# One scan chain in the S5 stage, more buffers there, adaLN by TensorE alone, and the convolutions of q, k and v where their projections end

## The chip, the core and the metric

The kernel runs on one core of one Trainium2 chip. The metric is the time of one execution on the device in microseconds (us). The core's engines are TensorE (PE, matmul), its weight load (PEld), VectorE (DVE), ScalarE (ACT), GpSimd (POOL) and SyncE (SP, which issues most DMAs). Each engine carries out its own instructions in one fixed order and waits on semaphores for the others.

## The reference, cut to what matters

One layer of a diffusion trunk: 512 latent tokens and 256 context tokens of width 2048, all float32.

```
mod = silu(c) @ ada_w + ada_b                    # adaLN, 6 parts of 2048
hin = concat([ctx*(1+csc1)+csh1, x*(1+sc1)+sh1]) # 768 tokens
proj = hin @ w_in                                # u | q | k | v | z | a,b
s5   = s5_mixer(u)      # 64 groups, bidirectional diagonal complex scan, gelu, gate
q, k, v = silu(short_conv(q,k,v))                # 5 taps along the tokens, per channel
dn   = gated_delta_rule(l2norm(q), l2norm(k), v) # 8 heads of 128, chunks of 64, both directions
x = layer_norm(ALPHA*x + g1 * (concat(s5, rms(dn)*silu(z)) @ w_out))
x = layer_norm(ALPHA*x + g2 * expert_choice_ffn(x*(1+sc2)+sh2))   # 16 experts, SwiGLU
```

The context tokens enter through the scans only; the output is the latent stream. g1, sh2, sc2 and g2 are four of the six adaLN parts, 2048 columns each, made in 16 chunks of 512 columns.

## The kernel before, in words

Matrix products that must be exact to float32 are made by splitting a weight tile in two: `split_w` (L380) loads `wr` by DMA, casts it to `wh` on ACT (L388) and subtracts to get `wl` on POOL (L390); `mm3` (L394) then makes three matmuls, L396 to L398. `proj_store` (L422) uses this for one head of q, k, v or z: 16 steps of 128 rows, 512 latent columns in the PSUM tile `pl` and, for k and v, 256 context columns in `pc`, copied by ACT to a tile `ue` and sent to DRAM (`pj`).

The program runs through these stages. `phase_in` makes the first adaLN parts and the S5 inputs u, which `put_u` sends to DRAM. The S5 stage follows: `s5_lags` (L1104 and others, mostly DVE), `s5_states` (matmuls L1133, 32 steps of two groups), `s5_scan` (94 dependent steps of three DVE operations, L1156 to L1158; `CHAINS` cuts the 64 groups into chains that are scanned apart), `s5_local`, `s5_outputs` (16 steps: two ACT copies `Hs`, L1188 and L1189, then 16 matmuls, L1192), `s5_gelu`, and `gates` (ends in six transposes, L495). The projections of k and v for 8 heads and the first six of q and z (`PRE`) stand after it in the source; the tool that sets each engine's order mixes their matmuls into the S5 stage, wherever it expects PE to be free.

Then the DeltaNet stage: ten iterations, in each of which `merge` interleaves `dn_front` for one head, `dn_inverse` and `dn_values` for the head before, `dn_scan` for the one before that, and up to four of the remaining projections (`REST`: four of q, six of z). `dn_front` and `dn_values` load the raw k, q, v from `pj` and call `conv_silu`: one ACT scaling, four DVE multiply-adds (L511) for each part, one ACT tanh and one DVE multiply (L514). The first PE work of the stage is L572, the transposes of the finished k of head 0. The same stretch holds the S5 gate product, the output projection (`mix_parts`) and the adaLN chunks that are left. `ada_rest` makes 16 chunks; four are made early (`NN`), of which two by `ada_vec`, on DVE, and 12 come in the DeltaNet stage. Each chunk by `ada_chunk` is 8 DMAs of 512 KB and 16 matmuls (L217) of 512 columns with 32 weights each, in four groups of PE columns.

The rest of the program, from L1370 on (router, experts, final norm), is bound by PE and by the experts' weights, and the change does not touch it.

Of the kernel before, what the change touches and what calls it, by code (L numbers as in the profile page):

```python
# [11 lines left out]
F32 = mybir.dt.float32  # L12
# [193 lines left out]
def ada_chunk(K, I, pool, c0, nk=8, bufs=2):  # L206

    nc = K.nc
    src = I["ada_w"]
    pa = mp(K, (128, 512), K.adb)  # L210
    for k0 in range(0, KT, nk):
        aw = pool.tile([128, nk, 512], F32, name="aw", tag="aw", bufs=bufs)
        nc.sync.dma_start(aw, ap(src, c0 + k0 * 128 * 6 * D, [[6 * D, 128], [128 * 6 * D, nk], [1, 512]]))
        for kk in range(nk):
            k = k0 + kk
            j = k % 4
            nc.tensor.matmul(pa[32 * j:32 * j + 32], K.cT[:, k], aw[:, kk], start=k < 4, stop=k >= 12, tile_position=(0, 32 * j))  # L217
    return pa
# [12 lines left out]
def ada_cols(K, I, pool, c0, dst, m, **kw):  # L231

    nc = K.nc
    pa = ada_chunk(K, I, pool, c0, **kw)
    pm = mp(K, (128, 512), K.adb)[:, :4 * m].rearrange("p (a b) -> p a b", a=4)
    turn(K, pool, pa, pm)
    cb = c0 // 128
    nc.vector.tensor_tensor(dst, pm, bc(K.cols[:, cb:cb + 4][:, :, None], [128, 4, m]), op=ADD)
    yield from ()


def ada_vec(K, I, pool, c0, dst, m, nk, bufs):

    nc = K.nc
    V = nc.vector
    acc = pool.tile([128, 512], F32, name="part2", bufs=1)
    for k0 in range(0, KT, nk):
        aw = pool.tile([128, nk, 512], F32, name="aw", tag="aw", bufs=bufs)
        nc.sync.dma_start(aw, ap(I["ada_w"], c0 + k0 * 128 * 6 * D, [[6 * D, 128], [128 * 6 * D, nk], [1, 512]]))
        for kk in range(nk):  # L250
            c = K.cT[:, k0 + kk, 0:1]
            if k0 + kk == 0:
                V.tensor_scalar(acc, aw[:, kk], c, None, op0=MUL)
            else:
                V.scalar_tensor_tensor(acc, aw[:, kk], c, acc, op0=MUL, op1=ADD)
        if AVY:
            yield
    t = pool.tile([128, 512], F32, name="part", bufs=1)
    V.transpose(t, acc)
    r = pool.tile([128, 16, 1], F32, name="part3", bufs=1)  # L260
    V.tensor_reduce(r[:, :, 0], t.rearrange("p (a c) -> p a c", c=32), axis=AX.X, op=ADD)
    pm = mp(K, (128, 4, 1), K.adb)
    for q in range(4):
        nc.tensor.matmul(pm[32 * q:32 * q + 32], K.sel32, r.rearrange("p (a q) m -> p q a m", q=4)[:, q], start=True, stop=True, tile_position=(0, 32 * q))
    cb = c0 // 128
    V.tensor_tensor(dst, pm, K.cols[:, cb:cb + 4][:, :, None], op=ADD)
# [155 lines left out]
def proj_store(K, I, which, h):  # L422

    nc = K.nc
    ctx = which in (1, 2)
    S = Ctx()
    yield from proj_steps(K, I, 1024 + 1024 * which + 128 * h, ctx, S)
    n = NT if ctx else NL
    e = K.up.tile([128, NT], F32, name="ue", bufs=2)
    nc.scalar.copy(e[:, :NL], S.pl)  # L430
    if ctx:
        nc.scalar.copy(e[:, NL:], S.pc)
    nc.sync.dma_start(K.pj[8 * which + h][:, :n], e[:, :n])
# [68 lines left out]
def conv_silu(K, col, parts, out, th, eng):  # L502

    nc = K.nc
    N = sum(n for _, _, n in parts)
# [7 lines left out]
    nc.scalar.activation(th[:, :N], out[:, :N], AF.Tanh)  # L513
    nc.vector.scalar_tensor_tensor(out[:, :N], th[:, :N], 1.0, out[:, :N], op0=ADD, op1=MUL)  # L514
# [12 lines left out]
def dn_raw(K, which, h, n):  # L527
    t = K.dn.tile([128, NT], F32, name="raw", bufs=2)
    K.nc.sync.dma_start(t[:, :n], K.pj[8 * which + h][:, :n])
    return t  # L530


def dn_front(K, h, S):
# [4 lines left out]
    raw = dn_raw(K, 1, h, NT)  # L538
    rawq = dn_raw(K, 0, h, NL)
    kr = dn.tile([128, NT], F32, name="kr")  # L540
    conv_silu(K, 8 + h, [(raw[:, :NL], 0, NL), (raw[:, NL:], NL, NC)], kr, raw, V)
    yield
# [34 lines left out]
    S.qT = qT = dn.tile([128, NL], F32, name="qT", bufs=2)  # L577
    conv_silu(K, h, [(rawq[:, :NL], 0, NL)], qT, rawq, V)
    yield
# [3 lines left out]
    for j in range(4):  # L583
        A.activation(rawq[:, NL:NL + 128], pt[:, j, :], AF.Square, accum_out=ss[:, 6 + j:7 + j])
# [41 lines left out]
def dn_values(K, h, S):  # L626
# [3 lines left out]
    rawv = dn_raw(K, 2, h, NT)  # L630
# [3 lines left out]
    vr = dn.tile([128, NT], F32, name="vr")  # L634
    conv_silu(K, 16 + h, [(rawv[:, :NL], 0, NL), (rawv[:, NL:], NL, NC)], vr, rawv, nc.vector)
    yield
# [241 lines left out]
AV = (2, 3)  # L878
AVY = 0
# [7 lines left out]
NKA = (2,3)  # L887
# [6 lines left out]
NKB = (2,3)  # L894

CHAINS = ((0, 32, "vector"), (32, 32, "vector"))
# [6 lines left out]
def transposed(K, p, src, n, dst):  # L903
# [4 lines left out]
    t = p.tile([128, n, 128], F32, name="tpd", bufs=2)  # L908
# [395 lines left out]
def ada_rest(K, I):  # L1304
# [4 lines left out]
    for s, dst in zip(range(2, 6), cols):  # L1309
        for ch in range(4):  # L1310
            f = ada_vec if 4 * (s - 2) + ch in AV else ada_cols
            yield from f(K, I, K.ada, s * D + ch * 512, dst[:, 4 * ch:4 * ch + 4], 1, nk=K.nka[0], bufs=K.nka[1])
# [365 lines left out]
def hybrid_trunk_kernel(tc, I, O):  # L1678
# [3 lines left out]
    with ExitStack() as es:  # L1682
# [39 lines left out]
        def put_u(i, pl, pc):  # L1722
            ue = K.up.tile([128, 8, 96], F32, name="ue", bufs=2)
# [6 lines left out]
        with left("acc") as accp:  # L1730
            uts, par = phase_in(K, I, accp, s5k)
            for i, (pl, pc) in enumerate(uts):
                put_u(i, pl, pc)
# [4 lines left out]
        K.banks = dict(mp=4, pp=3, ada=1)  # L1738
# [167 lines left out]
```

## Time and profile before

| what | value |
|---|---|
| median of 3 runs | 2703.14 us (2702.12 to 2708.47) |
| the profiled execution | 2703.15 us, span 2701.4 us |
| busy over the span | PE 91%, PEld 57%, DVE 48%, POOL 29%, ACT 27% |
| mean granted clock of TensorE | 0.959 of full |
| last matmul of the S5 states (L1133) starts | 574.9 us |
| last scan operation (L1158) starts | 687.2 us |
| last matmul of the S5 outputs (L1192) starts | 714.8 us |
| first matmul of the DeltaNet stage (L572) starts | 805.3 us |
| first matmul of the router (L1370) starts | 1555.5 us |

The landmarks cut the span into stages: up to 574.9 the inputs, lags and states; to 687.2 the scan; to 805.3 outputs, gelu and gates; to 1555.5 the DeltaNet stage with the output projection; from there the mixture of experts. All times below are microseconds from the span's start unless they are marked ns.

### The profile page before, as it was taken

Reading aid. Unit: us, or ns where it says so; the run is one execution under the profiler, and the core shown is the slowest. Engines: PE = TensorE matmul, PEld = TensorE weight load, DVE = VectorE, ACT = ScalarE, POOL = GpSimd, SP = SyncE. Lnnn points to the kernel's source line nnn. Section 1 sums busy time; section 2 is a strip of 40 time slices with the busy share of each in tenths; the row PEclk is TensorE's granted clock in tenths of the full one; section 3 lists DMA queues with packets and bytes.
Section 4 is the critical chain, followed back from the end, with each engine's and each line's share of the span. In section 5 each row is a group of like instructions: output and inputs, shape, how many; then the busy total and the mean of one; then the engine's idle time right before and its main releaser. Section 6 shows DMA issues by size and latency. Waiting matters only on the chain. (4 is left out here: it accounts for less than half of the span.)

```text
span 2701.4 us, 41223 instructions
## 1 busy us (share of the span) xinstructions
PE 2467.7 (91%) x16062; PEld 1541.3 (57%) x16062; DVE 1300.9 (48%) x2831; ACT 717.7 (27%) x1611; POOL 783.6 (29%) x747
## 2 busy tenths in 40 slices
PE   7998989899878989899999859999999999999994
PEld 4665778778756766566667724434444444444441
DVE  3362685899577677767877560411111101010106
ACT  2223233534544344443333330201010101010111
POOL 2341275631255464545454410400000000000002
PEclk9998999999988999899999979999999999999997
DMA  9956847766654456777763287998999999999893
GB/s 281 323 176 166 266 148 210 195 163 163 187 158 123 116 174 197 239 224 227 225 194 85 63 319 276 362 382 339 390 384 389 383 390 366 406 366 408 350 406 128
DMA packets 444317, 698.73 MB, mean 259 GB/s; under 512 B 91288, under 2 KB 271001, under 8 KB 443097
## 3 DMA queue, kind: packets, MB, share of 16 engines
q1 hardware_dynamic: 438745, 693.82, 74.6%
q10 hardware_dynamic: 5376, 2.26, 0.4%
q8 instruction: 127, 2.08, 0.3%
q14 instruction: 69, 0.57, 0.1%
HBM read 646.12 MB, written 49.87 MB: 258 GB/s over the span
## 5 line engine op out<-in xcount | busy, mean ns | idle before, releaser
L390 POOL TENSOR_TENSOR wl<-wr,wh 128x512 fp32r<-128x512 f32 (+2 forms) x248 | 335.2, 1354 | 609.3 <-ACT wh L388 577.9
L1522 PE MATMUL mp<-ws,selT 128*64 128x512 f32 x1992 | 468.9, 594 | 0.5 <-ACT selT L1461 0.5
L1522 PEld LDWEIGHTS mp<-ws,selT 128*64 128x64 f32 x1992 | 176.2, 137 | 265.7 <-issue 258.8
L1556 PE MATMUL mp<-ws,hT 128*64 128x512 f32 x896 | 298.2, 603 | 0.0
L1606 POOL TENSOR_TENSOR yp<-ypf,yp 128x512 fp32r<-128x512 f32 x31 | 39.7, 1280 | 875.0 <-ACT yp L1605 875.0
L388 ACT CAST wh<-wr 128x512 fp32r<-128x512 f32 (+2 forms) x249 | 150.5, 605 | 351.3 <-PE pp L397 140.1
L396 PE MATMUL pp<-hi,wh 128*128 128x512 f32 (+1 forms) x528 | 222.0, 420 | 18.4 <-ACT wh L388 18.4
L398 PE MATMUL pp<-hi,wl 128*128 128x512 f32 (+1 forms) x528 | 221.6, 420 | 16.3 <-POOL wl L390 16.3
L397 PE MATMUL pp<-lo,wh 128*128 128x512 f32 (+1 forms) x528 | 217.4, 412 | 0.0
L1528 DVE SCALAR_TENSOR_TENSOR hid<-hid,mp 128x512 f32<-128x512 f32 x16 | 11.0, 688 | 354.9 <-ACT hid L1527 354.1
L1604 DVE SCALAR_TENSOR_TENSOR ypf<-mp,gc,g2r 128x512 f32<-128x512 f32 x32 | 24.0, 751 | 318.5 <-issue 184.9
L1556 PEld LDWEIGHTS mp<-ws,hT 128*64 128x64 f32 x896 | 83.5, 136 | 141.9 <-issue 130.2
L1618 DVE TENSOR_TENSOR acc<-acc,pp 128x512 f32<-128x512 f32 x124 | 79.1, 683 | 162.7 <-PE pp L1616 162.7
L1458 PEld LDWEIGHTS pp<-oh,mixed 128*128 128x128 f32 x1024 | 123.5, 197 | 57.3 <-issue 57.3
L1461 ACT ACTIVATE selT<-pp,colB,colA 128x128 f32<-128x128 f32 x128 | 48.3, 457 | 341.8 <-PE pp L1458 341.8
L1458 PE MATMUL pp<-oh,mixed 128*128 128x128 f32 x1024 | 136.8, 287 | 1.3 <-DVE oh L1450 1.3
L398 PEld LDWEIGHTS pp<-hi,wl 128*128 128x128 f32 (+1 forms) x528 | 102.7, 195 | 49.1 <-POOL wl L390 25.3
L396 PEld LDWEIGHTS pp<-hi,wh 128*128 128x128 f32 (+1 forms) x528 | 104.0, 197 | 37.3 <-ACT wh L388 23.0
L397 PEld LDWEIGHTS pp<-lo,wh 128*128 128x128 f32 (+1 forms) x528 | 104.1, 197 | 18.3 <-issue 4.7
L1527 ACT ACTIVATE hid<-mp 128x512 f32<-128x512 f32 x16 | 9.6, 597 | 381.6 <-PE mp L1522 381.6
L217 PE MATMUL ada<-aw,cT 128*32 128x512 f32 x448 | 100.1, 633 | 11.8 <-DMA aw<-in_ada_w_dram 7.3
L396 PE MATMUL pp<-oph,wh 128*128 128x512 f32 x240 | 98.9, 417 | 6.7 <-DVE Z L666 3.5
(583 smaller groups left out, 4819.2 us busy)
## 6 DMA issues: line engine op xcount, KB each, us to landing
ws<-in_exp_w_dram SPq DMA_DIRECT2D x375, 1024.0 KB
aw<-in_ada_w_dram SPq DMA_DIRECT2D x184, 512.0 KB
wr<-in_w_in_dram SPq DMA_DIRECT2D x157, 256.0 KB
wr<-in_w_out_dram SPq DMA_DIRECT2D x52, 256.0 KB
cl<-CL SPq DMA_DIRECT2D x8, 1024.0 KB
P<-tp SPq DMA_DIRECT2D x32, 256.0 KB
B<-tb SPq DMA_DIRECT2D x32, 256.0 KB
CLo<-cl SPq DMA_DIRECT2D x16, 512.0 KB
```

The costliest lines, as they stand in the source:

```text
L217: nc.tensor.matmul(pa[32 * j:32 * j + 32], K.cT[:, k], aw[:, kk], start=k < 4, stop=k >= 12, tile_position=(0, 32 * j))
L388: nc.scalar.copy(wh, wr)
L390: (nc.vector if K.nsp % K.sv == 1 else nc.gpsimd).tensor_tensor(wl, wr, wh.bitcast(F32), op=SUB)
L396: T.matmul(out, wh, hi, start=st, stop=False, **kw)
L397: T.matmul(out, wh, lo, start=False, stop=False, **kw)
L398: T.matmul(out, wl, hi, start=False, stop=sp, **kw)
L1458: T.matmul(pg[:, j], K.y[:, k, b], ohf[:, b], start=(b == 0), stop=(b == 3))
L1461: A.activation(S.selT[:, k], pg[:, j], AF.Identity, scale=K.A[:, k:k + 1], bias=K.B[:, k:k + 1])
L1522: T.matmul(acc4[2 * w + c][64 * a:64 * a + 64], S.selT[:, k, 64 * a:64 * a + 64], ws[w, a][:, kk, 512 * c:512 * c + 512], start=(k == 0), ...
L1556: T.matmul(acc[c][64 * a:64 * a + 64], S.hT[:, f0 + f, 64 * a:64 * a + 64], ws[a][:, f, 512 * c:512 * c + 512], start=(f0 + f == 0), stop= ...
L1606: (nc.vector if end else nc.gpsimd).tensor_tensor(t[:, 1], y, t[:, 0].bitcast(F32), op=SUB)
L1618: K.nc.vector.tensor_tensor(K.acc[:, b, s], K.acc[:, b, s], ps, op=ADD)
```

## The change

Four parts. (1) `CHAINS` holds one chain of 64 groups in place of two of 32, so the scan has 94 steps of three DVE operations twice as wide, and begins when all 32 steps of `s5_states` are done. (2) `ada_vec` goes, all 16 chunks are made by PE; a DMA piece is 4 row blocks of 256 columns in place of 2 row blocks of 512, so each piece feeds four matmuls of 256 columns, one in each column group. The number of pieces and their size stay. (3) `conv_silu` for q, k and v is called in `proj_store`, on the PSUM tiles, and `pj` holds finished k, q and v, which the DeltaNet stage loads; tanh and last multiply are made for each part. z is copied as before. (4) `put_u` has 8 tiles `ue` in a pool of its own in place of 2, `tpd` 4 in place of 2; in the S5 stage PSUM is given out as 3 banks `mp` and 4 `pp` in place of 4 and 3.

```
-def ada_chunk(K, I, pool, c0, nk=8, bufs=2):
+def ada_chunk(K, I, pool, c0, bufs=3):
...
-    for k0 in range(0, KT, nk):
-        aw = pool.tile([128, nk, 512], F32, name="aw", tag="aw", bufs=bufs)
-        nc.sync.dma_start(aw, ap(src, c0 + k0 * 128 * 6 * D, [[6 * D, 128], [128 * 6 * D, nk], [1, 512]]))
-        for kk in range(nk):
-            k = k0 + kk
-            j = k % 4
-            nc.tensor.matmul(pa[32 * j:32 * j + 32], K.cT[:, k], aw[:, kk], start=k < 4, stop=k >= 12, tile_position=(0, 32 * j))
-    return pa
+    for c in range(0, 512, 256):
+        for k0 in range(0, KT, 4):
+            aw = pool.tile([128, 4, 256], F32, name="aw", tag="aw", bufs=bufs)
+            nc.sync.dma_start(aw, ap(src, c0 + c + k0 * 128 * 6 * D, [[6 * D, 128], [128 * 6 * D, 4], [1, 256]]))
+            for j in range(4):
+                nc.tensor.matmul(pa[32 * j:32 * j + 32, c:c + 256], K.cT[:, k0 + j], aw[:, j], start=k0 == 0, stop=k0 == 12, tile_position=(0, 32 * j),
+                                 skip_group_check=True)
...
-def ada_vec(K, I, pool, c0, dst, m, nk, bufs):
...
     yield from proj_steps(K, I, 1024 + 1024 * which + 128 * h, ctx, S)
...
-    nc.scalar.copy(e[:, :NL], S.pl)
-    if ctx:
-        nc.scalar.copy(e[:, NL:], S.pc)
+    if which < 3:
+        conv_silu(K, 8 * which + h, [(S.pl, 0, NL)] + [(S.pc, NL, NC)] * ctx, e, K.up.tile([128, NL], F32, name="uth"), nc.vector)
+    else:
+        nc.scalar.copy(e[:, :NL], S.pl)
...
-    nc.scalar.activation(th[:, :N], out[:, :N], AF.Tanh)
-    nc.vector.scalar_tensor_tensor(out[:, :N], th[:, :N], 1.0, out[:, :N], op0=ADD, op1=MUL)
+    for _, a, n in parts:
+        nc.scalar.activation(th[:, :n], out[:, a:a + n], AF.Tanh)
+        nc.vector.scalar_tensor_tensor(out[:, a:a + n], th[:, :n], 1.0, out[:, a:a + n], op0=ADD, op1=MUL)
...
-    raw = dn_raw(K, 1, h, NT)
-    rawq = dn_raw(K, 0, h, NL)
-    kr = dn.tile([128, NT], F32, name="kr")
-    conv_silu(K, 8 + h, [(raw[:, :NL], 0, NL), (raw[:, NL:], NL, NC)], kr, raw, V)
-    yield
+    kr = dn.tile([128, NT], F32, name="kr", bufs=2)
+    nc.sync.dma_start(kr, K.pj[8 + h])
+    S.qT = qT = dn.tile([128, NL], F32, name="qT", bufs=2)
+    nc.sync.dma_start(qT, K.pj[h][:, :NL])
...
-AV = (2, 3)
...
-CHAINS = ((0, 32, "vector"), (32, 32, "vector"))
+CHAINS = ((0, 64, "vector"),)
...
-    t = p.tile([128, n, 128], F32, name="tpd", bufs=2)
+    t = p.tile([128, n, 128], F32, name="tpd", bufs=4)
...
-            ue = K.up.tile([128, 8, 96], F32, name="ue", bufs=2)
+        def put_u(i, pl, pc, pool):
+            ue = pool.tile([128, 8, 96], F32, name="ue", bufs=8)
...
-        K.banks = dict(mp=4, pp=3, ada=1)
+        K.banks = dict(mp=3, pp=4, ada=1)
```

The order of PE's instructions changes with it. Line numbers after the change are lower by 20 to 36: L372 to L374 there are L396 to L398 here, L1156 is L1192, L472 is L495, L542 is L572. Before, on PE, one place in the S5 outputs (`Hs` is the scanned state, `hi` and `hic` the split input of the projections):

```order
L396 MATMUL pp<-hi,wh 128x512
L397 MATMUL pp<-lo,wh 128x512
L398 MATMUL pp<-hi,wl 128x512
L396 MATMUL pp<-hic,wh 128x256
L397 MATMUL pp<-loc,wh 128x256
L1192 MATMUL mp<-Hs,CLo 128x64 x16
L398 MATMUL pp<-hic,wl 128x256
```

After, on PE, from the first step of the outputs to the gates, with the twelve projection matmuls between them cut to their first three:

```order
L1156 MATMUL mp<-Hs,CLo 128x64 x16
L372 MATMUL pp<-hi,wh 128x512
L373 MATMUL pp<-lo,wh 128x512
L374 MATMUL pp<-hi,wl 128x512
...
L1156 MATMUL mp<-Hs,CLo 128x64 x112
L472 MATMUL mp<-ident,gb 128x128 x6
L372 MATMUL pp<-hi,wh 128x512
L373 MATMUL pp<-lo,wh 128x512
L374 MATMUL pp<-hi,wl 128x512
```

Before, the projection matmuls stand in several stretches between the steps of the outputs, and 232 of these follow the last L1192 and precede the first L572. After, 15 of the 16 steps follow 12 projection matmuls almost at one go, the six transposes of the gates come straight behind the last, and 24 projection matmuls stand between them and the DeltaNet stage's first transposes; everything else of k, v and `PRE` is ahead of the outputs.

On DVE, in the scan before (`VH` is the state, two numbers for two chains, `m` the product with the step's factor):

```order
L1156 TENSOR_TENSOR m_3909<-VH_3378,Lm 128x128
L1156 TENSOR_TENSOR m_4501<-VH_3379,Lm 128x128
L1157 TENSOR_TENSOR VH_3378<-VH_3378,m_3909 128x64
L1157 TENSOR_TENSOR VH_3379<-VH_3379,m_4501 128x64
L1158 TENSOR_TENSOR VH_3378<-VH_3378,m_3909 128x64
L1158 TENSOR_TENSOR VH_3379<-VH_3379,m_4501 128x64
```

and after (L1120 to L1122 are the scan, L487 is the multiply-add of the convolution):

```order
L1120 TENSOR_TENSOR m_4292<-VH_3442,Lm 128x256
L1121 TENSOR_TENSOR VH_3442<-VH_3442,m_4292 128x128
L487 SCALAR_TENSOR_TENSOR ue<-pp,cw,ue 128x510
L1122 TENSOR_TENSOR VH_3442<-VH_3442,m_4292 128x128
L487 SCALAR_TENSOR_TENSOR ue<-pp,cw,ue 128x511
L487 SCALAR_TENSOR_TENSOR ue<-pp,cw,ue 128x254
L1120 TENSOR_TENSOR m_4296<-VH_3442,Lm 128x256
L487 SCALAR_TENSOR_TENSOR ue<-pp,cw,ue 128x511
L487 SCALAR_TENSOR_TENSOR ue<-pp,cw,ue 128x255
L1121 TENSOR_TENSOR VH_3442<-VH_3442,m_4296 128x128
```

The other chain's operations have gone from between a step's operations, and multiply-adds of the convolution stand there.

In the DeltaNet stage PE has, before, pairs such as the first of these rows, 8 to a chunk (`glu` and `oph` are operands of the S5 gate and of the output projection):

```order
L217 MATMUL ada<-aw,cT 32x512 x2
L397 MATMUL pp<-opl,wh 128x512
L398 MATMUL pp<-oph,wl 128x512
L397 MATMUL pp<-opl,wh 128x512
L398 MATMUL pp<-oph,wl 128x512
```

and after:

```order
L216 MATMUL ada<-aw,cT 32x256 x4
L374 MATMUL pp<-glu,wl 128x512
L372 MATMUL pp<-glu,wh 128x512
L373 MATMUL pp<-glu,wh 128x512
L374 MATMUL pp<-glu,wl 128x512
```

A piece is now four matmuls of 256 columns, one per column group, still 8 pieces to a chunk.

## Rows read from the trace of the kernel before

**Rows 1.** Busy time by window: PE, PEld, DVE, ACT, POOL, clock, DMA share, GB/s.

```profile
575.00:687.00 112.00, 107.90 (x677) 96.95 (x676) 105.04 (x484) 37.73 (x53) 22.69 (x17) 0.95 0.71 168
687.00:805.00 118.00, 94.17 (x425) 73.11 (x424) 79.46 (x105) 57.61 (x85) 49.06 (x37) 0.91 0.60 169
805.00:1555.00 750.00, 686.11 (x6827) 506.03 (x6828) 538.73 (x1210) 298.86 (x777) 379.17 (x403) 0.95 0.57 170
```

**Rows 2.** Lines by instruction: duration ns min/median/max, first and last start.

```profile
L1133 PE MATMUL mp<-U,W x256: 243/275/530, 447.4 to 574.9; 128*128 128x96 f32 x128
L1158 DVE TENSOR_TENSOR VH<-VH,m x188: 208/213/1310, 512.1 to 687.2; 128x64 f32<-128x64 f32 x188
L1192 PE MATMUL mp<-Hs,CLo x256: 217/275/421, 652.8 to 714.8; 128*128 128x64 f32 x128
L572 PE MATMUL front<-ident,kr x48: 270/273/448, 805.3 to 1394.0; 128*128 128x128 f32 x48
L1370 PE MATMUL po<-yT,wrt x32: 592/605/617, 1555.5 to 1588.5; 128*32 128x512 f32 x32
```

**Rows 3.** Timeline of DVE, one step of the scan alone: start, duration, instruction.

```profile
681.36 0.29 DVE L1156 TENSOR_TENSOR m<-VH,Lm 128x128 f32<-128x128 f32 x1
681.69 0.22 DVE L1157 TENSOR_TENSOR VH<-VH,m 128x64 f32<-128x64 f32 x1
...
682.21 0.29 DVE L1156 TENSOR_TENSOR m<-VH,Lm 128x128 f32<-128x128 f32 x1
```

**Rows 4.** Timeline of DVE, a scan operation of both chains beside a POOL subtraction.

```profile
610.63 1.61 DVE L1156 TENSOR_TENSOR m<-VH,Lm 128x128 f32<-128x128 f32 x2
```

**Rows 5.** Timeline of POOL at the same time.

```profile
610.59 1.30 POOL L390 TENSOR_TENSOR wl<-wr,wh 128x512 fp32r<-128x512 f32 x1 [2.67 <-ACT wh L388]
```

**Rows 6.** The convolution's lines: busy us, mean ns, idle before.

```profile
L511 DVE SCALAR_TENSOR_TENSOR vr<-raw,cw,vr 128x510 f32<-128x510 f32 (+1 forms) x64 | 50.2, 824 | 3.7 <-ACT vr L507 3.6
L511 DVE SCALAR_TENSOR_TENSOR kr<-raw,cw,kr 128x510 f32<-128x510 f32 (+1 forms) x64 | 49.9, 813 | 3.7 <-ACT kr L507 3.7
```

**Rows 7.** Multiply-adds on DVE, from SBUF (L511) and from PSUM (L1294): min/median/max.

```profile
L511 DVE SCALAR_TENSOR_TENSOR vr<-raw,cw,vr x64: 468/736/1785, 810.8 to 1422.3; 128x510 f32<-128x510 f32 x16, 128x254 f32<-128x254 f32 x16, 128x511 f32<-128x511 f32 x16, 128x255 f32<-128x255 f32 x16
...
L1294 DVE SCALAR_TENSOR_TENSOR mixed<-pp,ada,mixed x48: 699/746/754, 1258.4 to 1552.4; 128x512 f32<-128x512 f32 x48
```

**Rows 8.** The ACT copy of half a step's state in the outputs.

```profile
L1188 ACT COPY Hs<-VH 64x512 f32<-64x512 f32 x16 | 17.7, 1107 | 9.7 <-PE mp L1192 6.9 <-DVE VH L1158 2.7
```

**Rows 9.** DVE alone in gelu and gates: busy, clock, DMA.

```profile
708.00:788.00 80.00, 61.15 (x80) 0.89 0.55 156
```

**Rows 10.** Who PE waited for between 700 and 800.

```profile
PE pp L396 <- ACT wh L388: 9.7, 5, 3.1
PE pp L398 <- POOL wl L390: 6.5, 9, 1.1
```

**Rows 11.** Timeline of PE, two projection matmuls in a row.

```profile
739.31 0.39 PE L396 MATMUL pp<-hi,wh 128*128 128x512 f32 x1
739.54 0.40 PE L397 MATMUL pp<-lo,wh 128*128 128x512 f32 x1
```

**Rows 12.** The adaLN lines by PE and by DVE: busy, mean ns, idle before.

```profile
L217 PE MATMUL ada<-aw,cT 128*32 128x512 f32 x448 | 100.1, 633 | 11.8 <-DMA aw<-in_ada_w_dram 7.3 <-DVE ada L238 4.4
...
L255 DVE SCALAR_TENSOR_TENSOR part<-aw,cT,part 128x512 f32<-128x512 f32 x30 | 27.5, 916 | 11.1 <-DMA aw<-in_ada_w_dram 10.4
```

**Rows 13.** Timeline of PE: two 512-column adaLN matmuls, and four of 256 in `phase_in`.

```profile
31.26 0.64 PE L284 MATMUL pp<-aw,cT 128*32 128x256 f32 x8 [0.20 <-DMA aw<-in_ada_w_dram]
31.83 0.50 PE L396 MATMUL tr<-hi,wh 128*128 128x512 f32 x1
...
262.01 1.05 PE L217 MATMUL ada<-aw,cT 128*32 128x512 f32 x4
262.99 0.42 PE L398 MATMUL pp<-hi,wl 128*32 128x512 f32 x1
```

**Rows 14.** Who PE waited for between 850 and 1550, the longest in total.

```profile
PE scan L796 <- DVE vn L792: 8.1, 5, 5.9
```

## What the change will do to the time

> **What bounds the kernel now.** I first cut the span into stages, because PE's 91% is an average over stages with different limits. From 805 to 1555 PE is busy 686 of 750 us and DVE 539 [rows 1]: the DeltaNet stage is bound by PE, with 64 us of idle time. From 575 to 687 two engines are nearly full, PE 107.9 and DVE 105.0 of 112 us [rows 1]: DVE carries the scan and PE the projections under it. From 687 to 805 PE still works 94 of 118 us [rows 1], because projection matmuls fill the outputs, gelu and gates. So before the change the serial S5 chain (lags, states, scan, outputs, gelu, gates) has PE work under all of it, and the reader should ask of each part of the change which of the two it lengthens, that chain or PE's total. The landmarks are the starts of five lines [rows 2]: states end 574.9, scan 687.2, outputs 714.8, DeltaNet begins 805.3, router 1555.5.
>
> **Up to the end of the states.** Eight `ue` and four `tpd` tiles take waits out of the path to the lags, and two early adaLN chunks no longer hold DVE for 30 multiply-adds, 27.5 us [rows 12]. Against this, three of the k and v convolutions now fall into the lags on DVE (below: 6 us each, 18 us), and the states, DVE and POOL work too, share DVE with more of them. I set gain against loss: states end at 573, near the 574.9 of now. Bounds: 20 us earlier if the convolutions find gaps, 15 later if they all queue ahead.
>
> **The scan.** One step of one chain of 32 groups takes 681.36 to 682.21, 0.85 us, in three operations: 0.29 us for 128 elements and 0.22 for 64 [rows 3], so 64 more elements are worth about 0.07 us. Twice as wide, the first operation gains 128 elements and the other two 64 each: 0.85 + 0.13 + 0.14 = 1.11 us by estimate, 94 steps make 104 us. Before, the 188 steps ran from 512.1 to 687.2 [rows 2], and the first chain overlapped the second half of the states; now the scan cannot begin before the last state. Two things lie in its way. First the convolutions that the new order puts between its operations: 33 multiply-adds of 510 or so columns, 22 of 255, 9 and 6 of the closing multiplies. From PSUM a 512-column one takes 0.746 us at the median [rows 7]; for the half I take 0.42 and 0.45, just below the shortest of 0.468 from SBUF [rows 7]. That is 24.6 + 9.2 + 6.8 + 2.7 = 43 us. Second POOL: two first operations (one for each chain) that meet a `wl` subtraction take 1.61 us [rows 4] while POOL works 1.30 [rows 5]; without it they would take some 0.5 us by the single one of 0.29 [rows 3], so about 1.1 us are lost each time; with some 43 subtractions due in this stretch, of which I let 7 in 10 hit a scan operation, 33 us. The scan then takes 104 + 43 + 33 = 180 us, 573 to 754, where it now ends 112 us behind the states. Bounds: 104 + 43 = 147 if POOL costs nothing, 205 if every subtraction hits and convolutions are hindered too.
>
> [...] The trace has 0.746 from PSUM beside 0.736 from SBUF, and no maximum over 0.754 where the SBUF one reaches 1.785 [rows 7]; the row goes into the sum.
>
> **Outputs, gelu, gates.** An output step needs both `Hs` copies, one after the other on ACT, 1.1 us each [rows 8]; I take the second, L1189, to cost the same, so 2.2 us and 16 steps make 35. Now the steps run while the second chain is still scanned, and end at 714.8 [rows 2]. After the change none can begin before the scan ends: 754 + 2 + 35 = 791. Gelu and gates follow. From 714.8 to 805.3 they have 90 us now, with DVE busy 61 of 80 [rows 9], while `wl` subtractions stretch DVE and PE waits 9.7 and 6.5 us for weights [rows 10]. In the new order hardly any projection is left for this stretch, so DVE runs undisturbed; I take 48 us, between 40 (two thirds of the 61 busy) and 61. Then come 24 projection matmuls at 0.23 us [rows 11], 5.5 us. L572 begins at 791 + 48 + 6 = 845, 40 us later than 805.3. PE stands nearly idle for some 80 us there, and that is the price: the work that used to fill it now stands ahead of the outputs, where DVE's scan, not PE, sets the pace. Bounds: 821 (+16, POOL free and gelu at 40) and 885 (+80).
>
> **From L572 to the router.** Three terms. The adaLN chunks: a piece of two 512-column matmuls holds PE 262.01 to 262.99, 0.98 us [rows 13], for it uses two of four column groups. A piece of the new shape stands in `phase_in`, four matmuls of 256 columns: 31.26 to 31.83, 0.57 us [rows 13]. 12 chunks of 8 pieces are in this stage, 96 x 0.41 = 39 us less of PE's time. Second, 22 projection matmuls, 5 us [rows 11], are done ahead of L572 that were not. Third, DVE loses at least the 100 us of k's and v's multiply-adds here [rows 6], of 539 [rows 1], and the closing multiplies and part of q's too. What that returns is bounded by PE's 64 us of idle time [rows 1]; of it only the waits on DVE, of which the largest group is 8.1 us in five waits [rows 14], can shrink, and head 0's wait for its convolution goes. I take 20 us, bounds 0 and 45. Against the gain stand the added DMA descriptors (1 KB rows for 2 KB): the queue had 0.57 of its engines busy [rows 1], so I take nothing, and 10 us if they come late. Sum: 39 + 5 + 20 = 64 us less, 750 to 686, L1370 at 1531.
>
> **Behind L1370** nothing changes: 1146 us.
>
> **The sum.** Profiled execution 2703.15 (span 2701.4 and 1.75 around it, the same as the median of 2703.14): 2703 + 40 - 64 = 2679 us.
>
> **The rivals.**
> - *More comes back in the DeltaNet stage.* DVE 539 of 750 is the second engine; with over 100 us off it, PE might wait for hardly anything: relief 45, and L572 only 28 later. 2703 + 28 - 89 = 2642. For it: PE's idle 64. Against: the waits in that stage are many and short, on ACT and DMA as well as DVE [rows 14].
> - *The adaLN pieces do not get shorter in place.* In the DeltaNet stage the pieces stand between other matmuls and wait for DMA (7.3 us of L217's idle time [rows 12]); if each still costs 0.98, the 39 us are gone: 2703 + 40 - 25 = 2718. Against: the 31.26 row has the very shape.
> - *The S5 chain is longer than I reckon (the other side).* Place: the scan. If every POOL subtraction hits and the convolutions wait on PSUM banks in turn, the scan ends near 794, L572 at 885: 2703 + 80 - 64 = 2719. It decides from the point where L572 starts later than 805 + 64 = 869. For it: 1.61 us for a pair that needs 0.5 [rows 3, 4]; against: the projections run out before the scan does, which leaves its last part alone.
> - *Both sides cancel.* L572 45 later and no relief from DVE: 2703 + 45 - 44 = 2704, no change that can be told. A measurement of this kernel tells a change from none at about 0.3%, 8 us.
>
> **Chances.** Forecast 0.50 (own range 2657 to 2696: L572 between 28 and 57 later, relief between 10 and 35), more comes back 0.12, adaLN pieces not shorter 0.10, longer chain 0.15, cancel 0.13. Under 2695 lie the first, all but a little, and the second: 0.60. Within 8 us of 2703: the cancel and edges, 0.15. Above 2711: the others, 0.25. The range 2640 to 2725 takes in all the rivals' times and leaves the ends of the bounds out.
>
> **What would show it.** Scan operations that start near 573 and end near 754, with gaps filled by L487; Hs copies back to back at 2.2 us a step; PE idle some 80 us between the end of the projections and L542; L542 at 845; pieces of L216 at 0.57 us; 686 us from L542 to the router; the router's part unchanged. It is wrong above all if PE's idle time around the outputs is over 110 us, if DVE's work in the lags pushes the states back beyond 590, or if the DeltaNet stage keeps its 64 us of idle time because another engine than DVE sets its pace.

## The result and the profile after

The changed kernel takes 2742.77 us at the median of 4 runs (2731.0 to 2749.06) beside 2704.14 of the kernel before: 1.0136 times as long, interval 1.0094 to 1.0177. It is slower where the forecast said faster. The profiled execution took 2737.34 us, with a span of 2735.6, so the profiles show 34 of the 39 us between the medians. Here and below medians are over all executions of a run, and ratios and intervals leave out one execution each of a1, c3, d3 and e2, and one of the kernel before, that fell in a slower state.

The lines that answer to [rows 2], by instruction (duration in ns min/median/max, first and last start), are the states, the scan, the outputs, the first DeltaNet transposes and the router:

```profile
L1097 PE MATMUL mp<-U,W x256: 243/275/529, 447.1 to 576.6; 128*128 128x96 f32 x128
L1122 DVE TENSOR_TENSOR VH<-VH,m x94: 274/293/1389, 580.1 to 758.0; 128x128 f32<-128x128 f32 x94
L1156 PE MATMUL mp<-Hs,CLo x256: 221/421/447, 760.6 to 816.4; 128*128 128x64 f32 x128
L472 PE MATMUL mp<-ident,gb x6: 421/421/447, 860.2 to 878.5; 128*128 128x128 f32 x6
L542 PE MATMUL front<-ident,kr x48: 269/272/329, 886.6 to 1389.5; 128*128 128x128 f32 x48
L1333 PE MATMUL po<-yT,wrt x32: 592/605/617, 1590.1 to 1623.1; 128*32 128x512 f32 x32
```

The accounts close. The states end 2 us later (576.6 for 574.9). L542 starts 81 us later than L572 did. From there to the router it takes 703.5 us for 750.2, 47 less. Behind the router there are 1145.5 us of span for 1145.9. 81 - 47 = 34 is the difference of the two spans, 2735.6 - 2701.4.

The windows that answer to [rows 1] are the scan, the outputs, gelu and gates, and the DeltaNet stage (PE, PEld, DVE, ACT, POOL, clock, DMA share, GB/s):

```profile
577.00:758.00 181.00, 169.27 (x868) 143.18 (x867) 165.26 (x354) 45.95 (x82) 54.98 (x41) 0.94 0.53 124
758.00:816.00 58.00, 51.82 (x277) 49.79 (x275) 10.34 (x22) 37.15 (x37) 4.35 (x4) 0.64 0.56 164
816.00:887.00 71.00, 10.67 (x38) 8.43 (x39) 46.12 (x79) 16.72 (x27) 5.26 (x6) 0.52 0.37 105
887.00:1590.00 703.00, 659.66 (x7189) 506.33 (x7187) 432.58 (x1063) 269.35 (x726) 359.97 (x407) 0.97 0.63 186
```

PE is busy 10.7 of 71 us in gelu and gates, where before it was busy 94 of 118 in the whole stretch [rows 1]; the granted clock is 0.52 there, for 0.91 before in the whole stretch [rows 1]. From the states' end to L542 PE is idle 78 us, the sum of the first three windows, where it was idle 28 before [rows 1]. The stretch that lost is read best from PE's timeline (start, duration, instruction, and in brackets the idle time and who ended it):

```profile
772.08 1.97 PE L1156 MATMUL mp<-Hs,CLo 128*128 128x64 f32 x16 [0.40 <-DMA CLo<-cl]
774.28 3.24 PE L1156 MATMUL mp<-Hs,CLo 128*128 128x64 f32 x16 [0.24 <-DMA CLo<-cl]
777.89 17.30 PE L1156 MATMUL mp<-Hs,CLo 128*128 128x64 f32 x80 [0.36 <-DMA CLo<-cl]
799.53 17.30 PE L1156 MATMUL mp<-Hs,CLo 128*128 128x64 f32 x80 [4.34 <-DMA CLo<-cl]
860.17 1.09 PE L472 MATMUL mp<-ident,gb 128*128 128x128 f32 x4 [43.34 <-DVE gb L468]
878.25 0.66 PE L472 MATMUL mp<-ident,gb 128*128 128x128 f32 x2 [16.99 <-DVE gb L468]
878.56 0.78 PE L372 MATMUL pp<-hi,wh 128*128 128x512 f32 x1
879.14 0.63 PE L373 MATMUL pp<-lo,wh 128*128 128x512 f32 x1
```

A step of 16 matmuls takes 1.97 us at 772, 3.24 at 774, and the last ten steps take 3.46 each (17.30 for five). On ACT the two `Hs` copies of a step take 2.13 us together, as forecast, but the next pair waits for PE:

```profile
788.46 1.07 ACT L1152 COPY Hs<-VH 64x512 f32<-64x512 f32 x1 [1.27 <-PE mp L1156]
789.53 1.06 ACT L1153 COPY Hs<-VH 64x512 f32<-64x512 f32 x1
791.87 1.06 ACT L1152 COPY Hs<-VH 64x512 f32<-64x512 f32 x1 [1.28 <-PE mp L1156]
```

So in the last ten steps PE at a granted clock of 0.50 (778.0 to 816.4), not ACT, sets the pace, 3.41 us from one copy to its like. Behind the outputs the chain that ended last (start, duration, what) goes through DRAM and back. The S5 output is written by eight DMA issues on SP, lands, is loaded again for gelu, and the gates do the same with their scan. These are pieces of that chain, the first two from within the outputs, the others between 822 and 864:

```profile
792.02 0.77 SPq L1161
...
792.89 6.51 DMA CLo<-cl
...
822.05 0.34 DVE Y L1157
...
828.53 4.45 DMA yd<-Y
...
833.05 5.04 DMA y<-yd
...
847.14 5.04 DMA y<-yd
...
859.94 2.29 DMA gsc<-gb
```

The load of CLo that PE waits 4.34 us for is issued at 792.9, right behind eight SP issues of the output's own write (L1161, 785.4 to 792.8). Between 822 and 864 PE is busy 1.1 of 42 us and DVE 32.4; the chain passes between DVE, SP's issues and the DMAs. Gelu and gates alone, from the last output step to the last transposes of the gates, before and after, and DVE's longest wait after:

```profile
714.80:782.80 68.00, 53.79 (x196) 39.78 (x194) 54.11 (x74) 25.79 (x41) 25.62 (x16) 0.87 0.52 140
816.40:878.50 62.10, 1.77 (x9) 1.24 (x9) 45.41 (x76) 14.79 (x21) 3.78 (x5) 0.50 0.31 86
868.82 0.28 DVE L456 TENSOR_SCALAR gz<-ge 64x256 f32<-64x256 f32 x1 [7.82 <-ACT ge L455]
```

In the DeltaNet stage PE's idle time fell from 64 to 43 us (703.0 less 659.7) and the adaLN line's busy time, in the same stretch, from 84.9 to 69.9 us:

```profile
L217 PE MATMUL ada<-aw,cT 128*32 128x512 f32 x384 | 84.9, 633 | 10.0 <-DMA aw<-in_ada_w_dram 5.5 <-DVE ada L238 4.4
L216 PE MATMUL ada<-aw,cT 128*32 128x256 f32 x768 | 69.9, 398 | 6.1 <-DVE ada L242 3.2 <-DMA aw<-in_ada_w_dram 2.8
```

### The profile page after: what moved, and what is told of

The parts are those of the page before. It is cut to its first block, busy times and chain, and to the rows that moved or that the text cites. A ratio compares the mean times of both kernels' runs of the same rounds, so it can differ in the third digit from the quotient of the medians.

```text
span 2735.6 us, 42075 instructions
## 1 busy us (share of the span) xinstructions
PE 2469.3 (90%) x16638; PEld 1568.4 (57%) x16638; DVE 1229.6 (45%) x2531; ACT 703.8 (26%) x1588; POOL 756.0 (28%) x747
## 4 chain that ended last, share of the span: by engine, by line
PE 65%; DVE 13%; DMA 11%; issue 4%; POOL 3%; ACT 2%; SPq 2%; DVEq 0%; ACTq 0%; POOLq 0%
PE mp L1485 17%; PE mp L1519 10%; PE pp L374 5%; PE pp L1421 5%; PE pp L372 5%; PE pp L373 5%; PE pp L1579 3%; DMA B<-tb 2%; DMA wr<-in_w_in_dram 2%; PE ada L216 2%; DVE Z L631 2%; DMA aw<-in_ada_w_dram 2%; DVE tp L630 1%; PE pp L260 1%; DMA us<-U 1%
## 5 line engine op out<-in xcount | busy, mean ns | idle before, releaser
L366 POOL TENSOR_TENSOR wl<-wr,wh 128x512 fp32r<-128x512 f32 (+2 forms) x248 | 323.9, 1308 | 569.5 <-ACT wh L364 521.9
L374 PE MATMUL pp<-hi,wl 128*128 128x512 f32 (+1 forms) x528 | 220.8, 418 | 20.8 <-POOL wl L366 20.6
L372 PE MATMUL pp<-hi,wh 128*128 128x512 f32 (+1 forms) x528 | 220.0, 417 | 5.6 <-ACT wh L364 5.6
L374 PEld LDWEIGHTS pp<-hi,wl 128*128 128x128 f32 (+1 forms) x528 | 102.9, 195 | 50.5 <-POOL wl L366 27.0
L487 DVE SCALAR_TENSOR_TENSOR ue<-pp,cw,ue 128x510 f32<-128x510 f32 (+3 forms) x160 | 96.7, 632 | 48.1 <-ACT ue L483 47.5
L372 PEld LDWEIGHTS pp<-hi,wh 128*128 128x128 f32 (+1 forms) x528 | 103.4, 196 | 24.6 <-ACT wh L364 8.1
L216 PE MATMUL ada<-aw,cT 128*32 128x256 f32 x1024 | 93.0, 403 | 12.9 <-DMA aw<-in_ada_w_dram 9.6
```

Of the source, the lines that this page charges most:

```text
L216: nc.tensor.matmul(pa[32 * j:32 * j + 32, c:c + 256], K.cT[:, k0 + j], aw[:, j], start=k0 == 0, stop=k0 == 12, tile_position=(0, 32 * j), ...
L366: (nc.vector if K.nsp % K.sv == 1 else nc.gpsimd).tensor_tensor(wl, wr, wh.bitcast(F32), op=SUB)
L372: T.matmul(out, wh, hi, start=st, stop=False, **kw)
L374: T.matmul(out, wl, hi, start=False, stop=sp, **kw)
L487: eng.scalar_tensor_tensor(out[:, a + d0:a + d1], p[:, d0 + o:d1 + o], K.cw[:, j, col:col + 1], out[:, a + d0:a + d1], op0=MUL, op1=ADD)
```

## The experiments

The theory after the result (A): the loss is the one chain, for it puts all of the outputs behind the whole scan, where no projection is left. Its rivals are in the expectations. The kernel before was run beside each group, at 2705.6 to 2708.2 us at the median. In every run the order of all instructions is made anew, so a part's effect includes that of the new order.

**One part undone on the changed kernel.** Four kernels.

```
a1  -CHAINS = ((0, 64, "vector"),)
    +CHAINS = ((0, 32, "vector"), (32, 32, "vector"))
a2  conv_silu back in dn_front and dn_values, proj_store copies by ACT
a3  ue and tpd 2 tiles again, K.banks = dict(mp=4, pp=3, ada=1)
a4  ada_chunk with pieces of [128,2,512], two chunks by ada_vec
```

> The changed kernel with two scan chains of 32 again, all else as changed. Theory A (the loss is the S5 tail: one long chain pushes outputs and gates behind all projections, so PE has nothing to do there, its clock falls and the outputs run at 3.4 us a step): the outputs begin before the second chain ends, the first DeltaNet transposes come some 40 us or more earlier than 887, and the time is about 2690. Rival B (the convolutions on DVE in the S5 stage are the loss, whatever the chains): the transposes stay near 880, about 2735. Rival C (DVE has the same work either way, so the end of the scan and of the gates stays): within 10 us of the changed kernel's 2743.

> The changed kernel with the convolutions of q, k and v back in the DeltaNet stage, one chain kept. Theory A: the scan loses its 43 us of convolution and ends near 720, but starts as late as changed and the DeltaNet stage gets its DVE work back (20 us of PE waits), so of the gain in the tail half is given back: about 2725. Rival B (the convolutions are the loss): first transposes near 820 and about 2690 or less. Rival C (no term of them matters): 2743.

> The changed kernel with the buffers and banks of before (2 tiles ue of u, 2 tpd, 4 banks mp and 3 pp). Theory A and rival B: the buffers are a side matter, the lags some 10 us later and the projections a little held back by 3 pp banks, which leaves more of them for the tail: 2730 to 2755. Rival D (4 pp banks let the projections run ahead and so empty the tail; with 3 they are held back): the tail fills again and the time is under 2715.

> The changed kernel with adaLN as before (pieces of two 512-column matmuls, two chunks on DVE). The traces so far: L217 held PE 84.9 us from 805 to 1555 before, L216 69.9 us after, so the new pieces save 15 to 20 us there, not the 39 of the forecast, because two pieces of before that lie side by side already take 1.00 us together. Theory A: about 18 us slower than the changed kernel, 2760. Rival E (the 39 us are saved and lost elsewhere): 2780 or more. Rival F (nothing saved): 2743.

| run | median us | to before (interval) | to the changed kernel |
|---|---|---|---|
| a1, two chains | 2700.68 | 0.9962 (0.9941 to 0.9984) | -42 |
| a2, no convolution there | 2727.8 | 1.0066 (1.0044 to 1.0088) | -15 |
| a3, old buffers and banks | 2724.67 | 1.0065 (1.0048 to 1.0082) | -18 |
| a4, old adaLN | 2763.11 | 1.019 (1.0158 to 1.0222) | +20 |

The last column is a difference of medians from two sittings, in which the kernel before stood at 2704.1 and 2705.9. Two chains give back more than the change lost: theory A, against B and C, though A had said 2690 and L542 40 us earlier or more, and it came 38 earlier. The landmarks of a1, the scan, the outputs and the first DeltaNet transposes (its line numbers are those of the changed kernel):

```profile
L1122 DVE TENSOR_TENSOR VH<-VH,m x188: 205/211/1316, 525.3 to 736.9; 128x64 f32<-128x64 f32 x188
L1156 PE MATMUL mp<-Hs,CLo x256: 221/275/323, 709.0 to 767.8; 128*128 128x64 f32 x128
L542 PE MATMUL front<-ident,kr x48: 270/273/472, 848.5 to 1360.3; 128*128 128x128 f32 x48
```

The scan ends 21 us earlier, but the outputs end 49 earlier (767.8 for 816.4), since they begin at 709.0, ahead of the second chain's end, and their matmul takes 275 ns at the median, not 421 (the granted clock is 1.00 from 737 to 768, and 0.64 over the outputs of the changed kernel). (Its profiled execution took 2711.78 us, 11 more than the median, so the profile shows 26 of the 42 us.) The convolution costs 15 us of the changed kernel as a2 has it, near A's 18, and B is out; A's place was off, since the scan ends at 690 in a2 and not near 720. The adaLN term is 20 us, near the 18 expected. The buffers were a loss of 18 here, which no theory had foretold: A and B said 2730 or more. Rival D, under 2715 with a filled tail, is half right. In a3 the states end at 563.5, 13 us earlier. The outputs do fill with projections (PE busy 55.8 of 57 us from 744 to 801, clock 1.00) and still take 54 us, for PE is now full; gelu and gates stay empty (PE busy 11.0 of 74 us, clock 0.54 from 801 to 875), and L542 comes at 874.8, 12 earlier.

**Filling the tail, and parts alone.** The fill was tried by writing more projections ahead of the DeltaNet stage, the chain was put alone on the kernel before, and adaLN and convolutions were put there together.

```
b1  changed kernel   -NP = 6   +NP = 10
b2  before + new ada_chunk + conv_silu in proj_store
b3  b2               -NP = 6   +NP = 10
b4  before           -CHAINS = ((0, 32, ...), (32, 32, ...))   +CHAINS = ((0, 64, "vector"),)
```

> The changed kernel with 10 in place of 6 projections of q and z written ahead of the DeltaNet stage (NP), so that four more can fill PE's empty time at outputs and gates; they are 16 x 3 matmuls of 0.23 us each, 44 us of PE. Theory A (the changed kernel lost because PE stood empty in the tail): the first DeltaNet transposes stay within 15 us of 887 while the DeltaNet stage gets up to 44 us shorter, 2700 to 2720. Rival G (the added weight subtractions on POOL and PE's work stretch the tail by as much as the later stage saves): 2735 to 2750.

> The kernel before with two parts of the change alone, adaLN by TensorE in the new pieces and the convolutions in the projections; chains, buffers and banks as before. If the parts add up as the runs so far say (two chains: 42 us better than the changed kernel; buffers of before: 18 better), 2743 - 42 - 18 = 2683, some 22 faster than before. If the buffers only cost where one chain stands, as with two chains the tail is filled anyway: 2701, no difference from before.

> The same two parts on the kernel before, and 10 projections of q and z ahead of the DeltaNet stage. Theory A, with the tail as the place where PE is idle: a further 15 to 30 us less than without, about 2660 to 2670. Rival G: no better than without, or worse.

> The kernel before with one scan chain of 64 groups as the only change. By the step of 1.11 us and no convolutions in the way, scan 575 to some 710, outputs to 755. Theory A: outputs and gates later by some 40 us and projections used up ahead, first transposes near 840, nothing gained behind: about 2735, 30 slower than before. Rival H (the chain costs only together with the convolutions on DVE): within 10 us of 2706.

b4 took 2745.53 us, 1.0152 (1.0137 to 1.0167): the chain alone makes as much as the change lost, +38, and needs no convolution for it (against H). Its scan, outputs and DeltaNet start, and the windows of its outputs and of gelu and gates:

```profile
L1158 DVE TENSOR_TENSOR VH<-VH,m x94: 291/293/1377, 571.8 to 707.6; 128x128 f32<-128x128 f32 x94
L1192 PE MATMUL mp<-Hs,CLo x256: 218/275/476, 710.1 to 773.8; 128*128 128x64 f32 x128
L572 PE MATMUL front<-ident,kr x48: 270/273/474, 856.8 to 1440.0; 128*128 128x128 f32 x48
```

```profile
708.00:774.00 66.00, 62.90 (x371) 56.99 (x372) 7.66 (x18) 42.01 (x44) 13.25 (x11) 0.87 0.58 172
774.00:857.00 83.00, 20.10 (x63) 14.96 (x63) 61.91 (x97) 27.56 (x48) 22.06 (x16) 0.59 0.42 121
```

The scan ends 20 us later than in the kernel before, the outputs 59 later, the DeltaNet stage begins 51 later. Theory A needs a correction here: projections are left for the outputs (PE busy 62.9 of 66 us, clock 0.87, the outputs' matmul 275 ns at the median), and it is gelu and gates that stand empty (20.1 of 83 us, clock 0.59). What one chain does in both kernels is to let no output begin before the whole scan is done. b1 took 2720.02 (1.0052, 1.0034 to 1.0069), 23 us less than the changed kernel, at the edge of A's band. The fill did not shorten the tail. L542 came at 898.8, 12 later, and the DeltaNet stage shrank from 703.5 to 672.7; four projections are 44 us of PE by the expectation's price, and the tail took them in at 12. b2 came to 2705.31 (0.9995, 0.9983 to 1.0007), no difference from before; of the two forms of its expectation the second holds, that the buffers cost nothing with two chains. b3 is slower, 2726.03 (1.0068, 1.0042 to 1.0094), as rival G had it: in b2 the tail holds projections, and four more only wait in it (by the profiles, which show 8 of the 21 us, DeltaNet begins at 901.9 for 849.6, while the stage gains 43).

**The other three parts alone.**

> The kernel before with adaLN by TensorE in the new pieces as the only change. Undoing it in the changed kernel cost 20 us, and nothing of the S5 chain is touched: theory A gives 2706 - 20 = 2686, DeltaNet stage 20 us shorter. Rival I (the gain needs the tail or the DVE relief of the convolutions, since in the kernel before the stage also waits on DVE): within 8 us of 2706.

> The kernel before with the convolutions in the projections as the only change. Adding up (with adaLN it gave 2705, adaLN alone 20 less than nothing): about 2725; the scan ends some 42 us later as with both, first transposes near 850, the DeltaNet stage some 22 us shorter than 750. Rival I: the convolution is what shortened the stage, and the time is near 2706.

> The kernel before with the buffers and banks as the only change. With one chain and convolutions they cost 18 us, with two chains and convolutions they gave about 4: I expect 2695 to 2712. If the cost is in the lags (states began 14 us later with them), it shows here too: 2715 to 2725.

> AdaLN by TensorE and the buffers and banks together on the kernel before, two chains, convolutions in the DeltaNet stage. Sum of c1 and the buffers' 4 us of gain: about 2682. If the buffers cost in the lags: 2700.

| on the kernel before | median us | to before (interval) | DeltaNet begins | stage to router |
|---|---|---|---|---|
| c1, adaLN | 2717.33 | 1.0034 (1.0017 to 1.005) | 833.5 | 734.1 |
| c2, convolutions | 2726.26 | 1.0071 (1.0053 to 1.0089) | 857.3 | 723.7 |
| c3, buffers and banks | 2708.12 | 1.0003 (0.9988 to 1.0018) | 810.4 | 746.9 |
| c4, adaLN and buffers | 2713.26 | 1.0027 (1.0009 to 1.0044) | 834.1 | 739.9 |

c1 misses: A's sum said 2686, and rival I, within 8 us of 2706, misses by less. The stage got 16 us shorter, as it should, but began 28 later. c4 misses both of its numbers, 2682 and 2700; c2 is near the 2725 of adding up, and c3 within its range. c1's window behind the gates:

```profile
777.00:833.00 56.00, 40.64 (x134) 29.98 (x133) 30.09 (x31) 19.16 (x38) 34.34 (x26) 0.82 0.45 133
```

The gates end at 777, earlier than before, but now 134 projection matmuls stand in PE's order between them and the first DeltaNet transposes where 48 stood, 56 us with PE busy 41; c4, with the same 134, begins at 834.1. So what adaLN saves is given back by where the projections came to stand. The parts do not add up: alone they make +38.4, +10.5, +19.5 and +1.3, 70 in sum, and the change is +38.6. adaLN and convolutions together (b2) stand at -2 where their sum is +30, so each seems to gain only in the order that the other brings; that is argued, for no run separates order from work.

**Which effect of the chain.** Chains of unequal width, on the kernel before (d1, d2) and on the changed one (d3).

```
d1  -CHAINS = ((0, 32, "vector"), (32, 32, "vector"))   +CHAINS = ((0, 48, "vector"), (48, 16, "vector"))
d2  the same with ((0, 16, "vector"), (16, 48, "vector"))
d3  d1's chains on the changed kernel
```

> The kernel before with chains of 48 and 16 groups. If the outputs behind the scan's end are what costs (theory A1): the scan ends within 10 us of 687 and 4 output steps in place of 8 are left, the time is 5 to 10 us below 2706. If the late start costs (A2): the first chain starts after 24 states near 543, the scan ends 10 to 20 us later and the time is 2715 to 2725.

> The kernel before with chains of 16 and 48 groups. A1: the last chain alone takes some 0.98 us a step, 92 us behind the states, so the scan ends near 690 as before, and 12 output steps in place of 8 are left: 10 to 20 us above 2706. A2: an early start and an end no later than before: within 8 us of 2706.

> The changed kernel with chains of 48 and 16 groups in place of one of 64; with 32 and 32 it took 2701. A1: no slower than that, 2690 to 2700. A2: between the one chain's 2743 and 2701, near 2715.

They took 2725.04 (1.0062, 1.0043 to 1.0081), 2731.61 (1.0084, 1.0062 to 1.0105) and 2716.31 (1.0046, 1.0026 to 1.0066). d1 and d3 fit A2's numbers; d2 is above both of its own. The outputs of d1 and of d2:

```profile
L1192 PE MATMUL mp<-Hs,CLo x256: 217/275/422, 680.6 to 741.3; 128*128 128x64 f32 x128
```

```profile
L1192 PE MATMUL mp<-Hs,CLo x256: 217/275/477, 642.1 to 746.8; 128*128 128x64 f32 x128
```

d1's scan ends at 690.3, within 3 us of before, so the late start does not lengthen the scan as A2 had it; still the outputs end at 741.3, 27 later, and A2 had its time right by another way. A1 counted the steps that are left behind the scan, four, and was wrong too: what counts here is when the first chain is done and the outputs can begin. From first to last matmul they took 62 us before (652.8 to 714.8), 61 in d1, 64 in b4 and 56 in the changed kernel, wherever they began. In d2 they begin at 642.1 and end late, since 12 of the 16 steps wait for the second chain, which ends at 697.6. So 32 and 32 is the balance of the four divisions tried, and one chain is the worst of them.

**The buffers' 18 us.**

```
e1  changed kernel   -K.banks = dict(mp=3, pp=4, ada=1)   +K.banks = dict(mp=4, pp=3, ada=1)
e2  e1 with two chains
```

> The changed kernel with 4 mp and 3 pp banks as before, the 8 ue and 4 tpd tiles kept. If the banks make the 18 us (3 mp banks hold back lags and states, which began 14 us later): states begin near 433 and the time is about 2725. If the SBUF tiles make them: 2743, states from 447.

> The changed kernel with two chains and 4 mp and 3 pp banks. With 3 and 4 banks it took 2701, with all buffers of before 2705, so I expect 2695 to 2706; if the banks make the 18 us whatever the chains, 2683.

They took 2735.27 (1.0125, 1.0097 to 1.0153) and 2709.79 (1.002, 1.0001 to 1.0039). e1 lies between both expectations, states from 441.0: 8 of the 18 us by the banks, 10 by the tiles, by medians that differ by less than the changed kernel's own runs do (18 us from lowest to highest), so this stays open. e2 is above both of its numbers: with two chains the old banks are 9 us slower than the new ones of a1, and the two intervals do not touch. So the new banks lose with one chain and gain with two, and c3 shows neither on the kernel before, where the states begin at 447.4 with either set; the cause stays open.

The fastest version is a1, the changed kernel with two chains: 2700.68 us, 0.9962 of before, 5 us by the medians.

## Why the prediction was wrong

The forecast had L542 40 us later and the stage behind it 64 shorter; L542 came 81 later and the stage was 47 shorter. So 41 of the 58 us between the forecast 2679 and the profiled 2737 lie ahead of L542, and 17 behind it. None of the forecast's three signs of being wrong came: PE was idle 67 us from 758 to 887 and not over 110, the states ended at 576.6, and the DeltaNet stage did not keep its idle time.

**Scan: right, and by its terms.** It ends at 758.0 for a forecast 754, 181 us behind the states for 180. A late step alone takes 1.11 us, as forecast. Its three lines, the convolutions and the subtractions are in the window's groups (busy us, mean ns):

```profile
L1120 DVE TENSOR_TENSOR m<-VH,Lm 128x256 f32<-128x256 f32 x94 | 46.1, 490 | 2.6
L1122 DVE TENSOR_TENSOR VH<-VH,m 128x128 f32<-128x128 f32 x93 | 44.2, 475 | 2.7
L1121 DVE TENSOR_TENSOR VH<-VH,m 128x128 f32<-128x128 f32 x94 | 39.0, 415 | 2.6
L487 DVE SCALAR_TENSOR_TENSOR ue<-pp,cw,ue 128x511 f32<-128x511 f32 (+3 forms) x58 | 35.0, 627 | 4.3 <-ACT ue L483 4.3
L491 DVE SCALAR_TENSOR_TENSOR ue<-uth,ue 128x512 f32<-128x512 f32 (+1 forms) x15 | 9.3, 622 | 3.6 <-ACT uth L490 3.5
L366 POOL TENSOR_TENSOR wl<-wr,wh 128x512 fp32r<-128x512 f32 x41 | 55.0, 1346 | 124.4 <-ACT wh L364 121.4 <-DMA wr<-in_w_in_dram 3.0
```

35.0 + 9.3 = 44 of convolution for 43. The scan's lines are busy 46.1 + 44.2 + 39.0 = 129 us; 94 steps at the 0.42, 0.29 and 0.29 of a step alone would be 94, so the 41 subtractions stretch it by some 35, for the 33 forecast: 35 scan operations take 0.82 to 1.51 us beside one, more than the 7 in 10 allowed, and each costs a little less than the 1.1 us reckoned. The convolution's multiply-adds by tile, min/median/max in ns:

```profile
L487 DVE SCALAR_TENSOR_TENSOR ue<-pp,cw,ue x58: 463/734/747, 576.5 to 744.7; 128x511 f32<-128x511 f32 x17, 128x510 f32<-128x510 f32 x17, 128x254 f32<-128x254 f32 x12, 128x255 f32<-128x255 f32 x12
```

Reading PSUM cost nothing extra that shows: 734 ns at the median beside 736 from SBUF [rows 7]. By these rows a copy to SBUF first would have had nothing to save here.

**Outputs, gelu, gates: the step that failed.** The forecast set 2 + 35 us for the outputs, 48 for gelu and gates and 5.5 for the last matmuls. Each term was sized by the engine that does most of the work, as if nothing else set the pace.

The outputs were to go at ACT's 2.2 us a step. They took 58 us from the scan's end (758.0 to 816.4), 21 more. The last ten steps make 13 of these, since PE, with the projections used up, is granted 0.50 of its clock there and needs 3.46 us for a step's 16 matmuls; the wait for CLo makes 4; the rest lies in the first six steps, with twelve projection matmuls among them. Filled with projections, as in a3, the outputs take 54 us for PE's other work.

Gelu and gates were to shrink from 68 us (714.8 to 782.8, the last transposes of the gates) to 48 with DVE undisturbed; they took 62 (816.4 to 878.5), 14 more than forecast. DVE's own work there did fall, from 54.1 us to 45.4, but DVE waits for 17 of the 62 us, 7.8 of them in one piece before L456, for the trips through DRAM and for ACT. In none of the kernels tried did this stretch take less than the 59.9 us of b4 (773.8 to 833.7). The last matmuls took 8 us, not 5.5: at a granted clock of 0.50 they come every 0.43 us till 883.

With 4 us of the scan these make the 41 us between 845 and 886.6. The forecast named the empty tail and its 80 us, but it had no term for the clock in it, and of the 20 us it gave the tail for being undisturbed, 6 came. Its rival of a longer chain had the place of L542 right, 885, by a wrong mechanism: the scan was on time. With the 686 us of the forecast behind it, that rival's number was 2719; the rest is the next point. The forecast's bounds do not follow from its terms either: a scan of 147 us with gelu and gates at 40 gives L542 at 803, not 821, and the rival's scan end of 794 lies beyond the scan's own bound of 205 us, which is 778.

**DeltaNet stage: the mechanism right, one term mis-sized.** 703.5 us for a forecast 686. The relief of idle time was 21 us (64 to 43) for 20, and it came where the forecast put it: in a2, with the convolutions back in the stage, PE is idle 75 us there. The adaLN term is the one that was mis-sized. It was to give 39 us, 96 old pieces at 0.98 less 96 new ones at 0.57, or 94 less 55; the lines are busy 84.9 and 69.9 us in the stage, 15 apart, and a4 shows 20 on the whole kernel. The old pieces cost 9 less than priced. Two of them that stand side by side fill all four column groups and take 1.00 us together, as this row of the kernel before shows:

```profile
1036.14 1.06 PE L217 MATMUL ada<-aw,cT 128*32 128x512 f32 x8
1037.14 0.25 PE L686 MATMUL inv<-Zc,R 32*32 32x32 f32 x4
```

Its eight records are four matmuls. The busy time of L217, 100.1 us in [rows 12] for all chunks, already said so: 14 chunks of 8 pieces at 0.98 would be 110. The new pieces cost 15 more than priced. A whole one takes its 0.57 us, but in many places the new order puts other matmuls inside a piece, and the part that is left over takes nearly as long as a whole piece. Here the last of a piece's four matmuls (two records) stands apart from the other three and is busy 0.62 us:

```profile
1103.49 1.06 PE L216 MATMUL ada<-aw,cT 128*32 128x256 f32 x14
1104.49 0.66 PE L549 MATMUL front<-ident,qT 128*128 128x128 f32 x4
1105.08 0.62 PE L216 MATMUL ada<-aw,cT 128*32 128x256 f32 x2
```

Such parts make 29 of the line's 85 stretches in the stage and 18 of its 70 us. The rival that each new piece still costs 0.98 did not hold. 15 + 21 and the 5 us of projections done earlier make 41 of the 47 us; the other 6 go with matmuls that are a little shorter at a granted clock of 0.97 in place of 0.95 [rows 1], which no run separates.

**What the forecast left out.** Parts of a change whose order is made anew do not add up: c1 has a shorter stage and a later start, in an order that only the row listing shows. The chain alone is 38 us of loss (b4); the other three parts together are worth 5 of gain (a1).

## What to carry to other kernels

When a serial chain is covered by independent PE work, ask at which point of the chain the cover ends: if the change pushes the chain's last stages behind it, price them by the chain of what waits for what (DMA round trips, ACT, DVE, PE at the clock that it is granted there, 0.50 here), not by the busy time of one engine. Splitting a scan in two pays when a consumer can start on the first half, if that half comes early and leaves little for the second: 16 and 48 began the outputs first and still ended them late. One wide chain gives the early start up for fewer instructions. Before pricing a shorter packed matmul, divide the line's whole busy time by its pieces, for neighbours may already overlap (two old pieces took 1.00 us together here, and one alone 0.98), and look in the new order for pieces that are cut in two.

## What the runs showed of the hardware that was not expected

In the outputs, with the projections used up, PE's granted clock fell at 774, from 1.00 before to 0.50 from 775 on, after steps of 1.97 us with 0.2 to 0.4 us of idle time between them, and the 16 output matmuls then took 3.46 us. In gelu and gates, with PE busy 1.8 of 62.1 us, 0.50 was granted. It rose again at 884, from 0.50 (878.5 to 883) to 1.00 (884 to 887), with projection matmuls back to back before it, whose spacing went from 0.43 to 0.23 us there. Thirty-five DVE scan operations that met a POOL subtraction took 0.82 to 1.51 us in place of 0.29 or 0.43; two of them, of 1.4 us each, stand here, and [rows 4] has the like:

```profile
753.43 0.29 DVE L1121 TENSOR_TENSOR VH<-VH,m 128x128 f32<-128x128 f32 x1
753.75 1.37 DVE L1122 TENSOR_TENSOR VH<-VH,m 128x128 f32<-128x128 f32 x1
755.15 1.40 DVE L1120 TENSOR_TENSOR m<-VH,Lm 128x256 f32<-128x256 f32 x1
```

The convolution's multiply-adds, with PSUM as their source, were not stretched: ten of the 58 ran beside a POOL subtraction, and none took over 747 ns, while those with SBUF as their source reached 1785 [rows 7].

Four adaLN matmuls of 256 columns, one in each column group, are busy 0.64 us together [rows 13], and one that stands apart 0.62 (1105.08), so here three of the four cost almost nothing, 0.02 us, as long as they stand together.
